# Room accounting of background tasks in a static planner: smaller declared needs, and two pieces more in the bound

## The chip, the cores and the metric

The kernel runs on one NeuronCore of a Trainium2 chip. The metric is the device time of one execution in microseconds (us). Before the change three executions took 2984.54, 2984.85 and 2988.25 us, with a median of 2984.85 us.

## What is computed

One layer of a diffusion block on 2048 latent tokens of width 1024, with 256 context tokens that are read before them. One input projection feeds two groups of four heads each. Group A is an mLSTM matrix memory with chunks of 128 tokens, scanned forward and backward. Group B is gated linear attention (GLA) with chunks of 64 and a decay for each key dimension. Both start from the state that the context leaves. The heads' outputs are normed, gated, put through one output projection and then through a SwiGLU feed-forward part. Cut to what matters:

```python
fc = mixer_features(modulate(rmsnorm(h_ctx, g_mix[l]), shc1, scc1), *proj, 1, h_ctx.shape[1])
fx = mixer_features(modulate(rmsnorm(x, g_mix[l]), shx1, scx1), *proj, rows, GRID_W)
ctx_st = context_states(fc)
ox, _ = mixer_apply(fx, ctx_st, m_norm_g[l], g_norm_g[l], w_out[l])   # both scans, both directions
x = x + gx1 * ox
x = x + gx2 * swiglu(modulate(rmsnorm(x, g_ffn[l]), shx2, scx2), w_gu[l], w_down[l])
return rmsnorm(x, g_final)
```

## The kernel before, in words

The program is straight-line code, written by a Python planner. The foreground is a list of units (`unit(...)`, run by `run_units`): projections whose weights are split into two parts, with 24 matmuls of 512 columns for one unit and one block of 512 tokens. After every such step `after_step` (line 534) calls `tasks_step` (line 508), which lets background tasks write their next piece of code. The tasks are Python generators. A `yield` ends a task's piece for this step.

The background tasks are these, with the function names of the code:
- `bt_task` (kind b) makes the decays' running sums of 256 tokens for four GLA heads and stores them to `d_bt`. Its matmuls use the weights `w2`, which live in the last arena tile.
- `scan_ga` (kind g) makes the attention matrix of one GLA head and 256 tokens ahead of the states, for the first 1024 tokens, and stores it to `d_att`: 16 tasks. `scan_gb` finishes such a piece later. `scan_g` does both for the last 1024 tokens: 16 tasks.
- `state_g` (kind g) makes the states of one GLA head, forward and backward.
- `ctx_gates`, `ctx_state_m`, `ctx_state_g` do the context. `m_tables` (kind m) makes the gate tables of all mLSTM heads, through small round trips over `d_bg` and `d_mp` in memory.
- `state_m` (kind m) makes the states of one mLSTM head in ten steps and a backward pass. It stores them to `d_cf`, `d_ub` and `d_cb`. Head h needs `m_tables`, the context's state, the unit `conv_unit` of its key, and head h-1.
- `scan_m` (kind m) is one mLSTM head on 256 tokens: 32 tasks. Each loads two `d_nm` tables and two `d_wi` tables, a q, a k, a v and two states, and stores its result to `d_hn`.
- `mix` (kind x) joins eight heads' results of 512 tokens for the output projection. It waits for all scans of those tokens.

All of them take their buffers from one pool, `slots`: pieces of 128 by 258 floats, two in each of 16 arena tiles. `take` (line 237) takes the piece that has been free longest and `free` puts it back at the end, so the number of free pieces sets how soon a piece is written again. Thirty pieces are in the pool from the start and one of them holds `rmask` for good. The last arena tile belongs to `w2`; when the last `bt_task` has run, `more_slots` (line 1510) puts its two pieces into the pool.

A task declares how many pieces it may hold (`ROOM`, line 482). `tasks_step` starts a waiting task only if three things hold: its kind has fewer running tasks than `limit`, its dependencies are done, and its room and that of all running tasks together are at most `NSLOT - 3`, which is 29. A task in its last piece (`"tail"`) counts with at most 2. The kinds are gone through in the order f, n, x, b, g, m, and inside a kind by priority: `m_tables` has -1, the states have 0, `scan_ga` 2 or 3, `scan_m` and `scan_g` 4 to 7. The limit of kind g is 4 in the first stage, then 2, then 1 during the gate units, then 2. The limit of kind m is 1, and 2 during the gate units. Kinds b, g and m are held for a step when the planner's own count of VectorE work is more than 8 us (later 5) behind its count of TensorE work.

The order of the foreground is: context and first 1024 tokens of the projections, 38 steps or so; the last 1024 tokens of k, q, kq, v, gv with `conv_unit` in between, up to about 850 us of the trace; 32 steps of `gate_unit`, each with a store to `d_o`; 16 steps of `out_unit`; the feed-forward units; then the same from `out_unit` on for the other 1024 tokens. Loads go through SyncE's queue in the order that the framework's scheduler gives them.

```python
if sum(not x.tail for x in act_) >= limit[kind]:
    break
if t.room + sum(x.room for k in KINDS for x in active[k]) > NSLOT - 3:
    continue
if all(d.done for d in t.deps):
```

Of the kernel before, what the change touches and what calls it, by code (L numbers as in the profile page):

```python
# [43 lines left out]
NSLOT = 32  # L44
# [155 lines left out]
def block_kernel(ctx: ExitStack, tc: tile.TileContext, I, out):  # L200
# [50 lines left out]
    def renew(lo, hi):  # L251

        arena[lo:hi] = [arena_tile(i) for i in range(lo, hi)]
# [225 lines left out]
        modulate(k, ctxv[:, k], ctxv[:, k], TCX, bc_ctx, a1[:, 1], b1[:, 1], hc)  # L479


    ROOM = dict(bt_task=5, ctx_gates=5, ctx_state_g=4, ctx_state_m=5, m_tables=9, state_m=9, state_g=10, scan_m=7, scan_g=8, scan_ga=8, scan_gb=6)
    KINDS = ("f", "n", "x", "b", "g", "m")
    queue = {k: [] for k in KINDS}
    active = {k: [] for k in KINDS}
# [4 lines left out]
    def add(kind, g, *deps, prio=0):  # L490
        t = Task(g, deps, prio, ROOM.get(g.__name__, 0))
        queue[kind].append(t)
        queue[kind].sort(key=lambda t: t.prio)
        return t

    def advance(t):
        if t.wait:
            t.wait -= 1
            return
        try:  # L500
            v = next(t.gen)
            if v == "tail":
                t.tail, t.wait, t.room = True, YT, min(t.room, 2)
            elif v:
                t.wait = v - 1
        except StopIteration:
            t.done = True

    def tasks_step():
        hold[0] -= 1  # L510
        for kind in KINDS:
            if kind in PACED and hold[0] >= 0:
                continue
            act_ = active[kind]
            for t in sorted(act_, key=lambda t: t.prio):
                if kind in PACED and not t.tail and load.behind() > lim[0]:
                    continue
                advance(t)
            act_[:] = [t for t in act_ if not t.done]
            for t in list(queue[kind]):  # L520
                if sum(not x.tail for x in act_) >= limit[kind]:
                    break
                if t.room + sum(x.room for k in KINDS for x in active[k]) > NSLOT - 3:
                    continue
                if all(d.done for d in t.deps):
                    queue[kind].remove(t)
                    act_.append(t)
                    advance(t)
                    if t.done:
                        act_.remove(t)  # L530

    nstep, late, last, hold, lim = [0], [], [None], [0], [LIM]

    def after_step():
        old = pend.pop(0)
        pend.append([])
        for f in old:
            f()
        nstep[0] += 1
        for _ in range(2 if nstep[0] % ADR == 0 else 1):  # L540
            if ada_todo:
                ada_rest(ada_todo.pop(0))
        tasks_step()
        for f in late:
            f()
        late.clear()
# [157 lines left out]
    def bt_task(src, dst):  # L704
# [31 lines left out]
        if not bt_left[0]:  # L736
            more_slots()
# [772 lines left out]
    def more_slots():  # L1510

        renew(NSLOT // 2 - 1, NSLOT // 2)
        slots.extend(arena[-1][:, i] for i in range(2))

    def set_limits(g, m):
        limit["g"], limit["m"] = g, m
# [642 lines left out]
```

## Time and profile before

| | |
|---|---|
| median of three runs | 2984.85 us |
| the profiled execution | 2986.63 us, of which the span is 2984.9 us |
| PE (TensorE matmuls) busy | 2664.0 us, 89% |
| DVE (VectorE) busy | 1939.0 us, 65% |
| ACT (ScalarE) busy | 1355.5 us, 45% |
| POOL (GpSimd) busy | 1786.0 us, 60% |
| granted TensorE clock, mean | 0.945 |

Times in the rows are microseconds from the first instruction unless marked ns. PE is TensorE's matmuls, PEld its weight loads, SP the queue of SyncE that issues loads and stores. PEclk is the granted TensorE clock as a share of 2.4 GHz; the other level is 1.2 GHz. Shares of busy time are averages over stages with different limits, so the stages are read one by one.

### The profile page before, as it was taken

Reading aid. Unit: us, or ns where it says so; the run is one execution under the profiler, and the core shown is the slowest. Engines: PE = TensorE matmul, PEld = TensorE weight load, DVE = VectorE, ACT = ScalarE, POOL = GpSimd, SP = SyncE. Lnnn points to the kernel's source line nnn. Section 1 sums busy time; section 2 is a strip of 40 time slices with the busy share of each in tenths; the row PEclk is TensorE's granted clock in tenths of the full one; section 3 lists DMA queues with packets and bytes.
Section 4 is the critical chain, followed back from the end, with each engine's and each line's share of the span. In section 5 each row is a group of like instructions: output and inputs, shape, how many; then the busy total and the mean of one; then the engine's idle time right before and its main releaser. Section 6 shows DMA issues by size and latency. Waiting matters only on the chain.

```text
span 2984.9 us, 43626 instructions
## 1 busy us (share of the span) xinstructions
PE 2664.0 (89%) x13322; PEld 2229.4 (75%) x13322; DVE 1939.0 (65%) x3949; ACT 1355.5 (45%) x3180; POOL 1786.0 (60%) x2339
## 2 busy tenths in 40 slices
PE   7889898798988886787999999898997999998898
PEld 4778887587776775665777888676786788886777
DVE  7588889886964235668777744767647544447765
ACT  4665555445454444444555433433434333333333
POOL 5667643345455433756667555767766655557773
PEclk7989899899999997898999999999998999999999
DMA  6755433246567767863554422322572332224222
GB/s 256 233 173 168 155 113 112 82 142 206 175 206 211 204 200 186 254 189 97 140 135 131 139 94 85 128 73 81 172 249 83 127 111 84 85 78 143 73 63 85
DMA packets 301817, 426.85 MB, mean 143 GB/s; under 512 B 39310, under 2 KB 186158, under 8 KB 298896
## 3 DMA queue, kind: packets, MB, share of 16 engines
q1 hardware_dynamic: 294224, 405.88, 44.3%
q0 software_dynamic: 7360, 18.19, 1.8%
q8 instruction: 106, 1.74, 0.2%
q14 instruction: 127, 1.04, 0.1%
HBM read 313.38 MB, written 110.55 MB: 142 GB/s over the span
## 4 chain that ended last, share of the span: by engine, by line
PE 42%; DVE 11%; DMA 11%; issue 4%; POOL 3%; ACT 2%; SPq 1%; DVEq 0%; POOLq 0%; ACTq 0%
PE mm L194 39%; DVE area L194 5%; DVE arena L194 3%; DMA arena<-d_nm 3%; DMA arena<-d_wi 2%; PE ps L194 2%; DVE gm L194 2%; DMA d_hn<-arena 1%; POOL w L194 1%; ACT arena L194 1%; SPq L208 1%; DVE xall L194 1%; DMA area<-in_wgu_dram 1%; POOL arena L194 1%; DMA arena<-d_bt 0%
## 5 line engine op out<-in xcount | busy, mean ns | idle before, releaser
L194 PE MATMUL mm<-area,w 128*128 128x512 f32 (+2 forms) x8264 | 2001.4, 400 | 111.5 <-DVE area L194 40.3
L194 PEld LDWEIGHTS mm<-area,w 128*128 128x128 f32 (+1 forms) x8264 | 1562.7, 194 | 457.9 <-DVE area L194 43.1
L194 POOL TENSOR_TENSOR w<-area,w 128x256 fp32r<-128x256 f32 x572 | 455.1, 818 | 272.8 <-ACT w L194 254.1
L194 POOL TENSOR_TENSOR w<-wr,w 128x256 fp32r<-128x256 f32 (+2 forms) x484 | 407.4, 862 | 167.5 <-ACT w L194 151.0
L194 POOL TENSOR_TENSOR arena<-arena 128x128 f32<-128x128 f32 (+1 forms) x520 | 248.7, 502 | 154.6 <-DMA arena<-d_bt 44.6
L194 ACT CAST w<-area 128x512 fp32r<-128x512 f32 x286 | 176.9, 620 | 283.9 <-PE mm L194 257.2
L194 PE MATMUL ps<-arena,arena 128*128 128x129 f32 (+1 forms) x1392 | 215.6, 298 | 72.5 <-ACT arena L194 30.4
L194 PEld LDWEIGHTS ps<-arena,arena 128*128 128x128 f32 x1392 | 195.8, 208 | 96.1 <-ACT arena L194 37.3
L194 DVE TENSOR_TENSOR arena<-arena,arena 128x256 f32<-128x256 f32 (+2 forms) x209 | 143.9, 697 | 188.0 <-DMA arena<-d_wi 90.6
L194 PE MATMUL mm<-w,area 128*128 128x256 f32 x1728 | 245.3, 299 | 6.9 <-ACT gm L194 4.9
L194 DVE TENSOR_TENSOR area<-area 128x512 f32<-128x512 f32 (+2 forms) x230 | 168.9, 747 | 112.5 <-DMA area<-in_wgu_dram 62.1
L194 DVE SCALAR_TENSOR_TENSOR gm<-gm,pc 128x63 f32<-128x63 f32 (+5 forms) x408 | 232.1, 611 | 7.5 <-ACT gm L194 5.1
L194 PEld LDWEIGHTS mm<-w,area 128*128 128x128 f32 x1728 | 229.3, 204 | 8.9 <-ACT gm L194 5.1
L194 ACT CAST w<-wr 128x512 fp32r<-128x512 f32 (+3 forms) x272 | 158.0, 583 | 142.7 <-PE mm L194 70.2
L194 DVE SCALAR_TENSOR_TENSOR area<-mm,modc,area 128x512 f32<-128x512 f32 (+1 forms) x184 | 131.7, 722 | 92.0 <-PE mm L194 91.9
L194 DVE TENSOR_TENSOR gm<-mm,gm 128x512 f32<-128x512 f32 (+3 forms) x136 | 93.0, 684 | 146.3 <-PE mm L194 122.6
L194 ACT COPY gm<-mm 128x512 f32<-128x512 f32 (+3 forms) x215 | 123.0, 574 | 141.5 <-PE mm L194 121.7
L194 PE MATMUL ps<-arena,xall 128*128 128x64 f32 x896 | 129.9, 287 | 35.8 <-DVE xall L194 14.6
L194 PEld LDWEIGHTS ps<-arena,xall 128*128 128x128 f32 x896 | 123.9, 207 | 50.0 <-issue 19.6
L194 DVE TENSOR_TENSOR arena<-ps,arena 64x128 f32<-64x128 f32 x448 | 128.5, 287 | 49.6 <-ACT ps L194 44.1
L194 ACT ACTIVATE ps<-arena 128x256 f32<-128x256 f32 x224 | 85.0, 383 | 161.3 <-DVE xall L194 112.2
L194 DVE TENSOR_TENSOR xall<-ps,arena 64x128 f32<-64x128 f32 x448 | 129.3, 289 | 7.4 <-PE ps L194 0.6
(176 smaller groups left out, 3037.6 us busy)
## 6 DMA issues: line engine op xcount, KB each, us to landing
area<-in_wgu_dram SPq DMA_DIRECT2D x170, 256.0 KB, 2.7
d_ff<-gm SPq DMA_DIRECT2D x88, 256.0 KB, 2.0
arena<-d_ff SPq DMA_DIRECT2D x88, 256.0 KB, 2.8
wr<-in_win_dram SPq DMA_DIRECT2D x72, 256.0 KB, 3.7
area<-in_wada_dram SPq DMA_DIRECT2D x32, 512.0 KB, 4.5
wr<-in_wout_dram SPq DMA_DIRECT2D x64, 256.0 KB, 3.7
arena<-d_kq SPq DMA_DIRECT2D x112, 128.0 KB, 3.0
arena<-d_bt SPq DMA_DIRECT2D x80, 128.0 KB, 3.0
```

The lines of the kernel that those rows point to most:

```text
L194: return f(out, *args, **kw)
L208: return nc.sync.dma_start(o, i)
```

## The change

The declared needs of nine kinds of task become smaller, and the bound becomes a variable that grows by two when `more_slots` gives the pool its last two pieces. No instruction of any task changes; what changes is the step at which a task may start.

```diff
-    ROOM = dict(bt_task=5, ctx_gates=5, ctx_state_g=4, ctx_state_m=5, m_tables=9, state_m=9, state_g=10, scan_m=7, scan_g=8, scan_ga=8, scan_gb=6)
+    ROOM = dict(bt_task=4, ctx_gates=5, ctx_state_g=4, ctx_state_m=4, m_tables=6, state_m=6, state_g=7, scan_m=7, scan_g=7, scan_ga=6, scan_gb=5)
...
-                if t.room + sum(x.room for k in KINDS for x in active[k]) > NSLOT - 3:
+                if t.room + sum(x.room for k in KINDS for x in active[k]) > room_of[0]:
                     continue
...
+    room_of = [NSLOT - 3]
     nstep, late, last, hold, lim = [0], [], [None], [0], [LIM]
...
         renew(NSLOT // 2 - 1, NSLOT // 2)
         slots.extend(arena[-1][:, i] for i in range(2))
+        room_of[0] += 2
```

## Rows read from the trace of the kernel before

**Rows 1.** the page: span, and busy time, share and instructions of each engine

```profile
span 2984.9 us, 43626 instructions
...
PE 2664.0 (89%) x13322; PEld 2229.4 (75%) x13322; DVE 1939.0 (65%) x3949; ACT 1355.5 (45%) x3180; POOL 1786.0 (60%) x2339
```

**Rows 2.** windows by stage: us, PE, PEld, DVE, ACT, POOL busy (x), PEclk, DMA, GB/s

```profile
100.00:360.00 260.00, 227.14 (x1561) 213.58 (x1561) 207.76 (x525) 157.29 (x390) 183.19 (x275) 0.91 0.57 182
360.00:640.00 280.00, 238.28 (x1375) 207.65 (x1375) 242.09 (x565) 133.21 (x287) 115.38 (x176) 0.92 0.35 104
640.00:850.00 210.00, 190.95 (x1079) 164.88 (x1078) 164.88 (x344) 107.62 (x314) 108.13 (x158) 0.98 0.63 190
850.00:1220.00 370.00, 295.38 (x1506) 246.97 (x1505) 150.87 (x468) 168.60 (x542) 172.73 (x275) 0.90 0.71 205
1220.00:1385.00 165.00, 143.08 (x724) 118.31 (x724) 113.08 (x300) 82.12 (x213) 105.61 (x164) 0.95 0.66 195
1385.00:1740.00 355.00, 326.10 (x1695) 274.91 (x1694) 264.38 (x681) 178.69 (x471) 233.34 (x358) 0.95 0.44 128
1740.00:2985.00 1245.00, 1163.63 (x5070) 945.88 (x5068) 725.11 (x957) 479.75 (x872) 811.95 (x853) 0.97 0.33 107
```

**Rows 3.** tiles: DMA of one name, count, issue ns, first and last start us

```profile
L210 SPq DMA_DIRECT2D d_att<-arena x16: 319/326/2007, 182.2 to 620.0; - x16
...
L210 SPq DMA_DIRECT2D d_bt<-arena x32: 319/320/418, 132.1 to 547.1; - x32
...
L208 SPq DMA_DIRECT2D arena<-d_zg x2: 319/371/423, 511.5 to 523.5; - x2
...
L210 POOL DMA_DIRECT2D d_cf<-arena x32: 539/560/596, 662.7 to 1071.6; - x32
...
L210 SPq DMA_DIRECT2D d_cf<-arena x4: 319/350/383, 358.2 to 430.0; - x4
...
L208 SPq DMA_DIRECT2D arena<-d_nm x64: 319/382/806, 865.7 to 1582.8; - x64
```

**Rows 4.** the timeline of DVE and PE at 565 us: start, us, idle before

```profile
565.59 0.24 DVE L194 TENSOR_TENSOR_SCAN arena<-arena,mctx 4x16 f32<-4x16 f32 x1 [9.05 <-DMA arena<-d_bg]
...
566.52 8.41 PE L194 MATMUL mm<-area,w 128*128 128x512 f32 x24 [15.17 <-ACT gm L194]
```

**Rows 5.** prices: PE's timeline (start, us), then DVE's groups of 100:1650 by form

```profile
1186.48 2.50 PE L194 MATMUL ps<-arena,arena 128*128 128x129 f32 x20 [0.95 <-DVE arena L194]
...
1137.31 1.10 PE L194 MATMUL ps<-arena,xall 128*128 128x64 f32 x8 [1.17 <-ACT arena L194]
...
L194 DVE TENSOR_TENSOR xall<-ps,arena 64x128 f32<-64x128 f32 x416 | 120.0, 289 | 6.9 <-PE ps L194 0.6
...
L194 DVE COPY_PREDICATED arena<-lmask,ps 128x256 f32<-128x256 uint8 x204 | 88.9, 445 | 6.1 <-ACT arena L194 1.4 <-PE ps L194 1.3
...
L194 DVE SCALAR_TENSOR_TENSOR arena<-arena,wcb,ps 128x129 f32<-128x129 f32 x60 | 20.6, 344 | 14.2 <-ACT arena L194 11.5 <-DMA d_ub<-arena 1.6
```

**Rows 6.** 850 to 1220 in parts, as Rows 2, and two tiles' DMAs in them

```profile
850.00:1075.00 225.00, 196.24 (x1044) 164.21 (x1043) 87.95 (x260) 103.21 (x327) 114.68 (x184) 0.98 0.70 209
...
1075.00:1150.00 75.00, 53.95 (x262) 44.17 (x260) 26.51 (x86) 31.88 (x110) 25.09 (x42) 0.90 0.69 187
...
1150.00:1220.00 70.00, 45.19 (x202) 38.59 (x203) 36.41 (x122) 33.51 (x107) 32.96 (x49) 0.67 0.76 211
...
L210 SPq DMA_DIRECT2D d_o<-gm x25: 319/382/1386, 857.3 to 1068.3; - x25
...
L208 SPq DMA_DIRECT2D arena<-d_nm x16: 319/382/806, 865.7 to 1049.0; - x16
...
L210 SPq DMA_DIRECT2D d_o<-gm x5: 383/422/422, 1077.2 to 1143.3; - x5
...
L208 SPq DMA_DIRECT2D arena<-d_nm x10: 320/388/488, 1089.6 to 1145.4; - x10
```

**Rows 7.** waits of SP's queue, 850:1220: us in total, times, longest us

```profile
SPq L208 <- DMA d_hn<-arena: 27.5, 14, 5.5
```

## The prediction, made before the change was timed

> **What bounds the kernel now.** I read the page first [rows 1]: PE is busy for 2664 of 2984.9 us and no other engine for more than 65%. So PE sets the time, and what can be won is PE's idle time and the time in which it runs at the lower clock. Then I read the windows by stage [rows 2]. For each stage I call "lost" the idle time of PE plus (1 - PEclk) times the length; this is an upper measure, since the clock is also low while PE idles. It gives 33+23 = 56 us for 100:360, 42+22 = 64 for 360:640, 19+4 = 23 for 640:850, 75+37 = 112 for 850:1220, 22+8 = 30 for 1220:1385 and 29+18 = 47 for 1385:1740. All of these 332 us lie where background tasks run. After 1740 the change can alter nothing but addresses: all scans are over.
>
> The stages have different limits. In 360:640 DVE is busy for 242 of 280 us (86%), in 100:360 for 80%; there the conv and attention work of DVE sets the pace. In 850:1220 DVE is busy for 41% only, and the losses there fall into two halves [rows 6]. From 850 to 1075 25 gate steps pass (25 stores to d_o) at 8.8 us each, with 8 `scan_m` (16 loads of d_nm, two to each) and 29+4.5 us lost: 1.3 us a step. From 1075 to 1150 5 steps pass at 16.5 us each with 5 `scan_m`, and 21+7.5 us are lost: 5.7 us a step. In the first half a `state_m` holds one of the two m places; in the second two `scan_m` run side by side. From 1150 to 1220 the last scans and the first `mix` run, and 25+23 = 48 us are lost.
>
> **What the admission rule does now.** With the old numbers three `scan_ga` and a `bt_task` make 8+8+8+5 = 29, so the limit of four is never used. `m_tables` (9) beside two `scan_ga` and a `bt_task` makes 30, so it waits until the last `bt_task` has gone; the trace agrees, since its gate tables are loaded at 511.5 and 523.5 and the decays' last store is at 547.1 [rows 3]. With the new numbers four `scan_ga` and a `bt_task` make 28, and `m_tables` in its old company makes 6+6+6+4 = 22. So two things move; everything else that runs is held by `limit`, by dependencies or by VectorE's count, which don't change. The two pieces more matter only for tails of 2 that blocked a start for a step or two: counted at nothing, within the bounds below.
>
> **Prices.** PE at full clock takes 2.50/20 = 0.125 us for an f32 instruction of a scan and 1.10/8 = 0.1375 for a level of the attention [rows 5]; each f32 matmul is two instructions, each transpose one. A `scan_ga` has 28 levels' and 4 others: 4.4 us. A `scan_m` has 22: 2.8. A `state_m` has 64+16: 10. A `state_g` has 48: 6. A `scan_g` is a `scan_ga` and 10 more: 5.6. On DVE a `scan_ga` costs 28 x 0.289 + 7 x 0.445 = 11.2 us and a `state_m` 15 x 0.344 for its forward pass and as much again for the other: 10.3 [rows 5]. These amounts are only moved. The PE work of all stages together stays, so the sum is that of the losses, but I write it by stage so that it can be checked.
>
> **100:360, +17 us.** `d_att` is stored 16 times from 182.2 to 620.0 [rows 3]. Four in flight for three lets about three more scans end before 360: +13 us of PE, +34 of DVE. DVE then stands where 360:640 stands now, whose losses are 23% of its length against 21.5% here: +4. Bounds 0 (they fill idle time) to +34 (all of DVE's work on the path). Queued behind each extra scan's POOL subtractions are the weight splits, whose cover is the three weights loaded ahead.
>
> **360:640, -12 us.** These three scans leave (-13 of PE). `m_tables` starts when the third context state has gone: the four store from 358.2 to 430.0 [rows 3], so at about 406. Its wait goes with it: DVE waited 9.05 us for d_bg and PE 15.17 behind it [rows 4]; next to it stands conv work then as now, so I count no gain. Its tables took about 90 us; with seven steps at this stage's pace and the fourth context state behind it, the first `state_m` starts near 490 and not 640, and about 1.3 of them come into this stage (+13 of PE). DVE gets 34 - 13 = 21 us less: its share falls to 79%. The nearest rows with such a share are 100:360 and 640:850, with losses of 21.5% and 11%: between -4 and -34. I take -12.
>
> **640:850, +4 us.** One `state_m` for another, since each waits for the conv unit of its head; two thirds of a `state_g` more. Bounds -2 to +8.
>
> **850:1220, +13 us.** The last store to d_cf is at 1071.6 now [rows 3]. The heads follow their conv units, the last of which ends here at about 800, so I put the end of the last `state_m` eight gate steps into the stage, at some 920. From there two `scan_m` run in each step, for 24 to 25 steps and not for the last 7 to 10. That brings nine more `scan_m` into the stage (25 of PE) and one `scan_g` (6), and takes 1.35 `state_m` and 0.7 `state_g` out (-18): +13. Its losses: 7 steps at 1.3, 25 at x, and a `mix` whose scans end early enough to lie beside gate units, for which I put 15 of the 48. With x = 3.5, the middle between the two halves [rows 6], this is 9+88+15 = 112, as much as now. With x = 1.3 it is 55 less, with 5.7 55 more. No row is nearer: what runs is the second half's, but without `mix` near.
>
> **1220:1740, -40 us.** Nine `scan_m` and a `scan_g` fewer: -31 of PE, and of the 77 us lost here, for 13 `scan_m` and 15 `scan_g` and the start of the feed-forward units, a third of an even share (77/28.5 = 2.7) each, 0.9: -9. Bounds -31 to -58 (2.7 each).
>
> **Sum.** 17 - 12 + 4 + 13 - 40 = -18 us. The profiled execution has 2984.9 us of span and 1.7 around it, 2986.6, which is 1.8 above the median; 2985 - 18 gives 2967 for the median.
>
> **The rivals.** *Slower: two mLSTM scans side by side cost more than they save.* Each loads d_nm and d_wi just before it uses them, into pieces that have just been given back: SP's loads waited 27.5 us in 14 cases for d_hn's stores out of them [rows 7], and the weights of the next gate units are queued behind them on SP. If a step in that company keeps its 5.7 us, the stage is 13+55 = 68 longer, and the sum is +37: 3022. It decides from x = 3.5 + 18/25 = 4.2 on. For it: the row itself. Against it: in 1385:1740, with one `scan_m` beside two `scan_g`, only 47 us are lost in 355. The Trainium skill's page "Perfetto Trace Analysis" (Optimization Strategy) says that the same gap repeating on the engine that should be saturated can mean too little SBUF for the next tile; by that rule more tasks in the same pieces can only add gaps. The wait on d_hn's stores agrees with it. *No change: the room is not what holds.* The `scan_ga` exclude one another level by level (`xbusy`), and VectorE's count skips steps; then the stages before 850 stay as they are, and what is won after 1220 is lost before: within 6 us of now. *Faster still.* Early tables fill DVE-bound stages with work that needs little DVE, and x stays at 1.3: -18 - 55 = -73, 2912. The same page (same section) advises to interleave stages with different limits; [rows 2] show such stages, DVE at 86% and then at 41%, and by it this case would be the likely one.
>
> **How the numbers follow.** A measurement of this kernel can tell about 0.2%, 6 us, from no change. I give 0.42 to the forecast and its neighbourhood (-6 to -50), 0.08 to more, 0.17 to no change and 0.33 to slower. So faster 0.50, same 0.17, slower 0.33. The range goes from 2935 to 3015: it leaves out most of the 0.08 and the upper end of slower, about 0.1. The forecast's own range, without the other sign, is 2935 to 2979.
>
> **What would show it.** Right: the loads of d_zg before 420 and the last store to d_cf near 920; the last store to d_att well before 620; some 55 loads of d_nm between the first d_o store and the last, and not about 36; the last of them near 1400 and not 1582.8; the gate steps at about 12 us each from the end of the `state_m` on. Wrong: gate steps of 14 us and more over the whole second part, with PE's clock there near the 0.90 and 0.67 of the end of the stage now [rows 6]; or a last d_cf store that has hardly moved, which would mean that something other than room held the chain; or more idle PE in 100:360 than the 33 us of now, without a gain in 360:640.

## The result and the profile after

The changed kernel takes 3023.3 us (median of four, 3015.11 to 3025.26), against 2986.55 for the kernel before beside it: a ratio of 1.0114, 95% interval 1.0094 to 1.0134. It is 37 us slower, where 18 us faster was forecast. The profiled execution is the quickest of the four, 3015.11 us with a span of 3013.3, so its trace shows 28.4 of the 37 us. The diff lowers the needs of eight kinds of task, not of nine: those of `ctx_gates`, `ctx_state_g` and `scan_m` stay. The page again, as [rows 1]:

```profile
span 3013.3 us, 43639 instructions
...
PE 2672.7 (89%) x13322; PEld 2236.2 (74%) x13322; DVE 1953.2 (65%) x3949; ACT 1359.4 (45%) x3180; POOL 1785.4 (59%) x2339
```

The windows by stage of the changed kernel, with the columns of [rows 2]: length, busy time of each engine, granted clock, share of the DMA engines, GB/s.

```profile
100.00:360.00 260.00, 227.89 (x1557) 212.68 (x1556) 214.47 (x529) 153.70 (x381) 182.09 (x270) 0.91 0.56 175
360.00:640.00 280.00, 238.52 (x1338) 206.16 (x1337) 235.50 (x562) 144.16 (x334) 116.75 (x191) 0.92 0.41 123
640.00:850.00 210.00, 189.76 (x1125) 165.90 (x1124) 158.24 (x345) 106.93 (x314) 113.11 (x169) 0.98 0.68 201
850.00:1220.00 370.00, 289.81 (x1461) 240.92 (x1460) 155.34 (x484) 163.34 (x523) 152.94 (x230) 0.88 0.70 185
1220.00:1385.00 165.00, 128.70 (x653) 108.87 (x654) 91.82 (x283) 79.88 (x236) 93.65 (x149) 0.86 0.84 218
1385.00:1740.00 355.00, 330.40 (x1678) 276.69 (x1677) 289.50 (x662) 172.87 (x410) 243.45 (x376) 0.97 0.36 114
1740.00:2985.00 1245.00, 1177.20 (x5090) 956.60 (x5089) 721.15 (x933) 484.49 (x876) 815.25 (x859) 0.97 0.33 105
```

The gate units now end inside the fifth window, whose PE clock has fallen from 0.95 to 0.86. The tiles that mark the tasks and the stages, as [rows 3]:

```profile
L210 SPq DMA_DIRECT2D d_att<-arena x16: 319/320/1122, 180.2 to 567.1; - x16
...
L208 SPq DMA_DIRECT2D arena<-d_zg x2: 338/360/383, 404.3 to 404.7; - x2
...
L210 POOL DMA_DIRECT2D d_cf<-arena x32: 542/547/774, 537.4 to 960.2; - x32
...
L208 SPq DMA_DIRECT2D arena<-d_nm x64: 319/382/1407, 837.6 to 1352.9; - x64
...
L210 SPq DMA_DIRECT2D d_o<-gm x32: 319/384/1502, 878.8 to 1297.0; - x32
...
L210 SPq DMA_DIRECT2D d_x<-area x32: 319/327/462, 1302.5 to 2291.5; - x32
```

`m_tables` starts at 404 and not at 511, the last `state_m` ends at 960 and not at 1072, and the last `scan_m` loads at 1353 and not at 1583: the tasks moved as the diff says. In the time that this took, cut at the same places of the foreground in both kernels:

| stretch | before | after | difference |
|---|---|---|---|
| start to the first `d_o` store | 857.3 | 878.8 | +21.5 |
| first `d_o` store to the first `d_x` store (gate units, and the wait for the last scans behind them) | 359.5 | 423.7 | +64.2 |
| first `d_x` store to the first reload of `d_x` (1896.9, 1922.4) | 680.1 | 619.9 | -60.2 |
| from there on | 1088.0 | 1090.9 | +2.9 |

Here is what the second and third of these look like as windows, the kernel before first:

```profile
857.30:1216.80 359.50, 286.04 (x1471) 239.67 (x1472) 143.31 (x449) 164.66 (x532) 165.25 (x262) 0.91 0.71 204
1216.80:1896.90 680.10, 629.28 (x3117) 525.70 (x3116) 444.17 (x1071) 321.58 (x788) 432.79 (x643) 0.96 0.45 133
```

and the changed kernel:

```profile
878.80:1302.50 423.70, 320.16 (x1604) 267.20 (x1603) 171.57 (x547) 190.65 (x611) 183.66 (x269) 0.86 0.75 193
1302.50:1922.40 619.90, 587.18 (x2882) 490.81 (x2881) 416.61 (x931) 283.86 (x653) 399.11 (x602) 0.97 0.38 118
```

The scans that left the later stage gave back 60 us there and cost 64 in the gate stage; in this trace the 21.5 us ahead of it are most of the loss. The column to look at is the last: the gate stage moves about 200 GB/s in both kernels. Length times rate is 73.3 MB before and 81.8 MB after.

### The profile page after: what moved, and what is told of

It reads as the page before. It is cut to its first block, busy times and chain, and to the rows that moved or that the text cites. A ratio compares the mean times of both kernels' runs of the same rounds, so it can differ in the third digit from the quotient of the medians.

```text
span 3013.3 us, 43639 instructions
## 1 busy us (share of the span) xinstructions
PE 2672.7 (89%) x13322; PEld 2236.2 (74%) x13322; DVE 1953.2 (65%) x3949; ACT 1359.4 (45%) x3180; POOL 1785.4 (59%) x2339
## 4 chain that ended last, share of the span: by engine, by line
PE 42%; DVE 7%; issue 2%; POOL 2%; DMA 1%; ACT 1%; DVEq 0%; SPq 0%; POOLq 0%; ACTq 0%
PE mm L194 40%; DVE area L194 4%; PE ps L194 2%; DVE arena L194 1%; POOL w L194 1%; DVE gm L194 1%; POOL area L194 0%; DMA wr<-in_wgu_dram 0%; ACT w L194 0%; DMA gm<-d_x 0%; ACT area L194 0%; DVE xall L194 0%; DVE wr L194 0%; POOL arena L194 0%; POOL sm L194 0%
## 5 line engine op out<-in xcount | busy, mean ns | idle before, releaser
L194 DVE TENSOR_TENSOR arena<-arena,arena 128x256 f32<-128x256 f32 (+4 forms) x210 | 149.5, 721 | 201.5 <-DMA arena<-d_wi 109.4
L194 DVE SCALAR_TENSOR_TENSOR gm<-gm,pc 128x441 f32<-128x441 f32 (+5 forms) x408 | 233.1, 614 | 10.9 <-ACT gm L194 9.3
L194 POOL TENSOR_TENSOR arena<-arena,mneg 128x256 f32<-128x256 f32 x64 | 42.9, 673 | 175.5 <-DMA arena<-d_nm 143.6
```

Of the source, the lines that this page charges most:

```text
L194: return f(out, *args, **kw)
```

## The experiments

Each ratio is against the kernel before on the same chip; the runs were made on several chips, which differ (the kernel before has medians from 2973.6 to 2986.55 us on them), so ratios and not medians are compared between runs. The traces are of one execution each, and stretches of them carry these differences too. Unless a diff says otherwise, a kernel is the changed one with an edit. "Gate stage" is the stretch from the first `d_o` store to the first `d_x` store.

**One m task at a time in the gate stage.**

```diff
-    NGC, NMC = 1, 2
+    NGC, NMC = 1, 1
```

> The changed kernel, with one mLSTM task at a time during the gate units in place of two. Pairs theory (two scan_m side by side make each gate step wait for their tables): the 32 gate steps, 418 us from the first to the last d_o store in the changed kernel, fall to 340 to 360, the PE clock there is back near 0.97, and the scans left over run later at some 4 us each; in all 2985 to 3005. Early theory (the loss lies before 880 us, in the stages that got more scan_ga and m_tables): the gate steps fall too, but the total stays above 3005, since d_o still begins 20 us late and the later scans cost what they saved.

Measured: 2986.05 us, ratio 1.0014 (0.9998 to 1.0031). The early chain stays and the pairs go, and the time is back at that of the kernel before. The late start of the gates stays too (884.4 for 857.3); it is made up by a gate stage that holds fewer `scan_m` than that of the kernel before, 14 for 18. Its gate stage and the stretch behind it:

```profile
884.40:1193.30 308.90, 263.46 (x1363) 220.18 (x1361) 134.41 (x394) 141.82 (x443) 149.99 (x231) 0.95 0.68 199
1193.30:1889.00 695.70, 633.88 (x3123) 530.40 (x3124) 452.91 (x1084) 329.36 (x820) 435.80 (x639) 0.94 0.46 134
```

14 `scan_m` load here inside the stage and 27.5 in the changed kernel. The 13.5 cost (423.7 - 308.9)/13.5 = 8.5 us each inside, and (695.7 - 619.9)/13.5 = 5.6 outside: what is lost by moving one is the difference, 2.9 us.

**The later scans queued only when the gate units are through.** `do(scans_m, range(NH), range(4, 8))` moves to just ahead of the `need` that closes the gate stage.

> The changed kernel, with the scan_m of the last 1024 tokens offered only after the gate units, so that 16 scans and not 28 can run beside the gate units, still two at a time. Pairs theory in the form 'each pair costs the same wherever it runs': the gate steps lose in proportion, 418 falls to some 370, the 16 others cost it back beside the output projection; total 3005 to 3020. Pairs theory in the form 'beside gate units a pair costs 8 us more than one scan beside scan_g': 360 for the gate steps and 2975 to 2995 in all. Early theory: above 3000.

Measured: 2983.03, ratio 1.0001 (0.999 to 1.0013), with 16.5 `scan_m` in a gate stage of 339.6 us. Same reading. The form of the theory in which a pair costs the same wherever it runs (3005 to 3020) is out; the time lies in the other form's range.

**At most one `scan_m` begun in a step.**

```diff
+                if t.gen.__name__ == "scan_m" and began[0] == nstep[0]:
+                    continue
                 if all(d.done for d in t.deps):
```

> The changed kernel, with at most one scan_m started in a step, so that the two that run side by side are a step apart and their eleven loads each don't come in one burst. If the burst is what makes the steps wait: the gate steps fall from 418 to 380 or less and the total to 2980 to 2995. If it is the number of scans in a step, since the mean stays near one a step: 410 to 425, and 3010 to 3025.

Measured: 3013.32, ratio 1.0093 (1.0073 to 1.0113). The gate stage does not shorten (429.6 against 423.7, with 29 `scan_m` in it for 27.5). Lock-step is not what makes the stage long. (A `scan_m` has nine loads, not eleven.)

**Four pieces fewer in the pool, with the same order of the tasks.** Four pieces are taken out of `slots` for good, and the bound stays.

> The changed kernel with four pieces withheld from the pool and the bound kept, so that every task starts at the same step, and only the time between giving back a piece and writing it again is shorter. If loads waiting for pieces just given back (30.7 us of waits for d_hn stores in the gate steps) carry the loss: the gate steps grow by 30 us or more, the total to 3050 or more. If the tables' own time from issue to landing carries it: within 10 us of the changed kernel, 3013 to 3033.

Measured: 3024.26, ratio 1.0139 (1.0119 to 1.0158), beside the changed kernel's 1.0114 (1.0094 to 1.0134). The gate stage is 423.6 us with four pieces fewer, and the waits of SyncE's queue for stores of `d_hn` in it are 29.3 us, against 32.7 in the changed kernel. The prediction's rival had put the pairs' price down to pieces written again too soon: that reason finds no support.

**The two moves one at a time.** The kernel before with the smaller needs for the attention tasks alone, `m_tables` held in its old place:

```diff
-    ROOM = dict(bt_task=5, ..., m_tables=9, ..., scan_ga=8, ...)
+    ROOM = dict(bt_task=4, ..., m_tables=16, ..., scan_ga=6, ...)
```

> The kernel before, in which only scan_ga and bt_task declare their smaller needs (6 and 4), so that four scan_ga run at once as in the changed kernel, while m_tables declares 16 and so keeps its old place behind the last bt_task. The gate stage then holds the old tasks: four state_m and 17 scan_m. Theory of the pairs (the loss is the 11 scan_m that the early chain of the m tasks brings into the gate stage, and the gates' late start is that chain's own work moved ahead of them): gates begin near the 857.3 of before, the time is within 6 us of before, 2980 to 2992. Rival, four attention tasks at once make the stage of 400 to 520 us slower: gates begin 15 to 22 us later, and the time is 3000 to 3010.

Measured: 2992.24, ratio 1.0034 (1.0023 to 1.0044). The other half, the changed kernel with three attention tasks at once:

```diff
-    ROOM = dict(bt_task=4, ..., scan_ga=6, ...)
+    ROOM = dict(bt_task=5, ..., scan_ga=8, ...)
```

> The changed kernel with scan_ga and bt_task back at 8 and 5, so that three scan_ga run at once as before; m_tables and the state_m stay early (13 to 21 steps ahead of before), and 27 scan_m start in the gate stage in place of 29. Theory of the pairs: the gate stage stays about 80 us longer than before's and less than that comes back later, 3008 to 3028. Rival, the four attention tasks carry the loss: gates begin near 860 and the time is 2980 to 2998.

Measured: 2990.72, ratio 1.0028 (1.0014 to 1.0042). Neither theory had this: each half loses a third of a per cent and both together 1.1. The gates begin at 836.6 with four attention tasks alone, 20.7 us earlier than before, and at 864.2 with the early chain alone, 6.9 later; together 21.5 later. Why the two add up so badly ahead of the gates is not settled. What the first half won there it lost again: its gate stage, with 18 `scan_m` as before, is 18.8 us longer. It also moves more:

```profile
836.60:1214.90 378.30, 295.89 (x1517) 249.49 (x1515) 152.79 (x470) 173.72 (x566) 178.71 (x281) 0.89 0.73 205
```

378.3 us at 205 GB/s are 77.6 MB, 4.3 more than before, and at 205 GB/s these would take 21 us (an estimate).

**The loads one step ahead of their use.**

```diff
             Ds.append(Dt)
             Ws.append(W)
+        yield
+        for d in range(2):
...
```

> The changed kernel, in which a scan_m issues its six first loads one step before it uses them (one more yield between them and the additions on GpSimd). The task lasts a step longer, and so 19 scan_m start in the gate stage in place of 29, as the planner counts. By the price of a scan_m inside the gate stage (8.8 us: 418.2 - 294.6 over 27 - 13 scans, changed kernel against the one with one m task at a time) and outside it (5.4 us: 695.7 - 619.9 over the same 14), ten fewer inside are worth 34 us: 2990. Theory that the landing time of the tables makes a scan_m dear: PE's idle time in the gate stage falls further, below 0.8 us for each scan, and the time is 2955 to 2980. Rival, the tables' landing does not matter, since PE waits for the chain of small steps behind them: 2985 to 3000.

Measured: 2986.5, ratio 1.0015 (1.0002 to 1.0027), the rival's number. The gate stage takes 328.7 us for 67.7 MB (206 GB/s), the rate of the kernel before. The stage was no quicker for what it moved; it only moved less. But the edit is no test of the landing, since the step of lead did not hide it. The waits of DVE for `d_wi` in the gate stage (us in total, times, longest), in the changed kernel and in this one:

```profile
DVE arena L194 <- DMA arena<-d_wi: 97.5, 35, 7.0
...
DVE arena L194 <- DMA arena<-d_wi: 63.9, 24, 6.1
```

Over 27.5 and 18 `scan_m` that is 3.5 us for each in both.

**Plain rows in place of the tables.**

```diff
-            dma(chunks(Dt), d_nm[None, r0:r0 + 2].broadcast_to([P, 2, P]))
-            dma(chunks(W), d_wi[None, r0:r0 + 2].broadcast_to([P, 2, P]))
+            dma(chunks(Dt), I["ident"][:, None, :].broadcast_to([P, 2, P]))
+            dma(chunks(W), I["ident"][:, None, :].broadcast_to([P, 2, P]))
```

> The changed kernel, in which the loads of d_nm and d_wi (two rows handed to all 128 partitions) read 128 rows of a constant matrix in their place, of the same size into the same pieces, and the exponentials have no per-row bias; the mLSTM scans therefore compute something else, and no load waits for the tables' making. Order and count of the tasks stay. Theory that the landing time of these broadcast loads (6.0 to 6.6 us in the gate stage) makes a pair of scan_m dear: the loads land in about 3 us, waits of GpSimd and VectorE on them fall to less than half of 117.5 and 93.5 us, the gate stage is 30 to 60 us shorter, and the time is 2965 to 2995. Rival, landing is hidden or as slow with plain rows: 3012 to 3028.

Measured: 2946.53, ratio 0.9869 (0.9846 to 0.9893): 2.45 points of the ratio, some 73 us, below the changed kernel and quicker than the kernel before. The DMA issues of 850:1300 in the changed kernel (tile, queue, count, size of one, median us from issue to landing):

```profile
arena<-d_wi SPq DMA_DIRECT2D x56, 128.0 KB, 6.4
arena<-d_nm SPq DMA_DIRECT2D x55, 128.0 KB, 6.6
arena<-d_cf SPq DMA_DIRECT2D x28, 129.0 KB, 5.2
```

and in this one:

```profile
arena<-in_ident_dram SPq DMA_DIRECT2D x125, 128.0 KB, 3.7
...
arena<-d_cf SPq DMA_DIRECT2D x32, 129.0 KB, 3.3
```

The same number of bytes lands in little more than half the time, and other loads land sooner too.

**Sixteen copies of the tables.** The tables are stored sixteen times, and each group of eight partitions reads a copy of its own:

```diff
-        dma(d_nm, Mr[:, P:2 * P])
+        dma(d_nm.rearrange("j p t -> p j t"), Mr[:, None, P:2 * P].broadcast_to([P, NCP, P]))
...
-            dma(chunks(Dt), d_nm[None, r0:r0 + 2].broadcast_to([P, 2, P]))
+                src = d_t[:, r0:r0 + 2].rearrange("j r t -> j (r t)")
+                dma(t, src[:, None].broadcast_to([NCP, P // NCP, HB]))
```

> The changed kernel, in which m_tables stores d_nm and d_wi sixteen times, 64 KB each, and the load of a scan_m takes each group of eight partitions from a copy of its own in place of all 128 partitions from one place. The result stays that of the reference. Theory that the time of the tables' loads comes from 128 partitions reading the same rows: they land in about 3.7 us as the plain loads did, in place of 6.4 and 6.6, the gate stage is 60 to 70 us shorter than 418.2, and the time is 2945 to 2965, faster than the kernel before. Rival, what was gained with the plain loads came from the other data or from the missing bias of the exponentials (so not from the source addresses): landing stays above 5.5 us and the time is 3010 to 3035, the sixteenfold stores adding some us.

Measured: 2951.11, ratio 0.9925 (0.9909 to 0.994). The loads of the tables in 850:1300:

```profile
arena<-d_wi SPq DMA_DIRECT2D x62, 128.0 KB, 3.1
arena<-d_nm SPq DMA_DIRECT2D x62, 128.0 KB, 3.2
```

So it is the 128 partitions reading one place that is slow, not the data, the size or the missing bias. In the kernel before, with copies:

> The kernel before with the same sixteen copies. Theory that the slow landing costs only where two scan_m run side by side: five steps of 16.5 us fall to the 11 or so of their neighbours and the end of the gate stage gains a little, 2955 to 2970, so that with quick tables the change of the room is worth a little or nothing. Rival, every scan_m pays for its tables wherever it runs: 32 times 2.6 us (69.5 us of the gate stage over 27 scans with the plain loads), some 2900, and the change of the room loses with quick tables too. Rival, nothing but the source of the plain loads' gain was data: 2980 to 2995.

Measured: 2920.75, ratio 0.9821 (0.9804 to 0.9838), the quickest of the versions that leave nothing out, and quicker than both kernels. Scans pay for their tables wherever they run: of the 69.8 us by which the gate stage and the stretch behind it are shorter in the traces (317.0 for 359.5 and 652.8 for 680.1), 27.3 lie behind the gates. The change of the room stays 30 us (1 point of the ratio) behind with quick tables too. With one m task at a time:

> The changed kernel with one m task at a time during the gate units, and sixteen copies of the tables. By the theory that the tables' landing costs in pairs, this gains less by the copies than the changed kernel does: 2950 to 2978 (2986 without copies). If every scan_m pays wherever it runs, it gains as much as the changed kernel, some 75 us: 2905 to 2920.

Measured: 2926.74, ratio 0.9834 (0.9815 to 0.9854); it gains 1.8 points by the copies and the changed kernel 1.9. And the kernel before with plain rows:

> The kernel before, in which the loads of d_nm and d_wi read 128 rows of a constant matrix in their place, of the same size, and the exponentials have no per-row bias; the mLSTM scans therefore compute something else. Against the changed kernel with the same loads (2946.5) it gives the price of the change without slow tables. Theory that only pairs pay: 2955 to 2975, so the change would have won some 10 to 25 us. Rival, every scan pays: 2900 to 2920, and the change would have lost even so.

Measured: 2907.99, ratio 0.9781 (0.9767 to 0.9796), against 0.9869 with the change. My theory that only pairs pay for slow tables fell twice: they are a cost of their own, and what the change loses is something else. Both kernels with copies, the changed one first:

```profile
874.80:1243.60 368.80, 299.48 (x1613) 249.95 (x1611) 173.72 (x547) 190.76 (x612) 183.20 (x267) 0.93 0.72 220
1243.60:1859.70 616.10, 585.73 (x2879) 490.30 (x2879) 419.32 (x932) 285.46 (x655) 400.77 (x604) 0.98 0.37 120
```

and the kernel before with copies:

```profile
851.50:1168.50 317.00, 274.56 (x1469) 229.53 (x1469) 142.65 (x450) 164.61 (x534) 168.77 (x262) 0.94 0.75 230
1168.50:1821.30 652.80, 616.43 (x3114) 517.52 (x3113) 451.44 (x1069) 319.93 (x785) 438.50 (x643) 0.97 0.44 139
```

The gate stage costs 51.8 us more and the later one gives back 36.7. It also moves more again: 81.1 MB against 72.9.

**The same added loads at two places.** On the kernel before with copies, two pieces more are loaded in each of 32 steps and given back unread:

```diff
         nstep[0] += 1
+        if 101 <= nstep[0] < 101+32:
+            for b in range(2):
+                t = take()
+                dma(t, d_kT[0, :, hs_(b)])
+                free(t)
```

> The kernel before with sixteen copies (2920.75), in which each of the 32 steps of the gate units loads two more pieces of 128 KB from d_kT and gives them back unread: 8.4 MB, about what six scan_m load and store (ten transfers of 128 KB each), and no other work. Theory that the gate stage is short of transfers (its DMA engines are busy for 0.74 of the time, against 0.36 after the sixteenth d_x store): PE loses in the gate stage what six more scan_m would cost there by the two kernels with copies, 3.5 us each ((97.0 - 59.8) over 10.5 scans), so some 20 us, and the time is 2935 to 2950. Rival, a scan_m is dear there for its chain of small steps on GpSimd, ScalarE, VectorE and TensorE, not for its transfers: within 8 us, 2913 to 2929.

Measured: 2947.93, ratio 0.989 (0.9873 to 0.9907), 0.69 points or 20 us above the kernel without them. In the later place (140 in place of 101):

> As the kernel with two more loads in each gate step, but in the 32 steps from the sixth behind the gate units' last on. Theory of the transfers: where the DMA engines are busy for 0.36 the same loads cost 0 to 7 us (1.1 us for each of six scan_m there), 2918 to 2930, and less than half of what they cost in the gate stage. Rival, the loads cost through the order of SyncE's queue or through the pieces that they hold, which is the same in both places: as much as in the gate stage, within 5 us.

Measured: 2932.89, ratio 0.9845 (0.9821 to 0.9868), 0.24 points or 7 us, whose interval still meets that of no added loads. The windows of the first:

```profile
853.80:1210.10 356.30, 289.71 (x1474) 245.29 (x1473) 151.16 (x455) 166.09 (x533) 168.94 (x262) 0.90 0.76 230
1210.10:1857.60 647.50, 615.83 (x3114) 517.42 (x3113) 449.88 (x1069) 319.06 (x787) 433.84 (x644) 0.98 0.44 140
```

and of the second:

```profile
855.40:1175.30 319.90, 277.41 (x1467) 233.30 (x1467) 140.83 (x450) 164.11 (x534) 168.37 (x262) 0.93 0.75 229
1175.30:1837.60 662.30, 617.77 (x3114) 515.36 (x3113) 451.99 (x1069) 318.56 (x785) 432.51 (x643) 0.97 0.47 150
```

64 loads of 128 KB are 8.4 MB. In the gate stage the rate stays at 230 GB/s and the share of the DMA engines at 0.75 to 0.76; what gives is the length, by 39.3 us, and 8.4 MB at 230 GB/s are 36.5. In the later stage the rate rises from 139 to 150 GB/s and the length by 9.5 us. But the trace without added loads is of another chip and of the quickest of its four executions (2913.1 us, median 2920.75). Held against each other, the two kernels with loads, which ran on one chip, put the price at 36.4 us in the gate stage (356.3 and 319.9) and 14.8 in the later one (662.3 and 647.5). By the ratios it is 20 us and 7 of the whole time, and their difference of 0.45 points, 13 us, has an interval of 5 to 22. So loads without any work lengthen the gate stage, and by more than the later one (two to three times by these numbers); that is shown. That the DMA engines' rate is what they run into is not.

SyncE's queue and the pieces are not ruled out as causes, since the same loads do not meet the same queue in both places. Its waits for the landing of loads of `d_kT`, of which the gate stage without added loads has none (us in total, times, longest), in the gate stage of the first and in the later stage of the second:

```profile
SPq L208 <- DMA arena<-d_kT: 39.3, 24, 3.3
...
SPq L208 <- DMA arena<-d_kT: 25.1, 22, 2.1
```

These waits are of the edit's own making. And added up from the trace, SyncE spends about 194 of the 317.0 us of the gate stage issuing (415 loads and stores) without the added loads and 224 of 356.3 with them, but only 187 of 652.8 in the later stage without them. This queue is a rival to the engines' rate, and no run parts the two. From issue to landing the loads of the gate stage take much the same without the added loads and with them: 4.0 and 3.6 us for `d_nm`, 3.2 and 3.5 for `d_wi`, 3.4 and 3.6 for `d_kT`.

**One start in a step, with copies.**

> The changed kernel with sixteen copies (2951.11), in which only one scan_m may start in a step, so that the two that run side by side are a step apart and not in lock-step. Theory that two chains at the same point of their course collide on the engines: the gate stage loses 15 us or more less than 97, 2925 to 2938. Rival, the loss is the same in any phase, as without copies, where the same edit gave 3013.3 for 3023.3: 2940 to 2952.

Measured: 2946.16, ratio 0.9882 (0.986 to 0.9904), 0.43 points below the same kernel without the rule. Its gate stage is 367.4 us, against 368.8; in its profile the gain lies behind the gate stage (605.9 for 616.1). The theory of colliding chains wanted it in the gate stage.

**Copies, and the loads a step ahead, in the kernel before.**

> The kernel before with sixteen copies, in which a scan_m issues its six first loads one step before it uses them. If GpSimd's and VectorE's waits on the tables still hold TensorE, 2900 to 2912. If the landing is covered by now, the longer task costs as much as it brings (15 scan_m in the gate stage in place of 17, the last start at step 194 in place of 174): 2915 to 2930.

Measured: 2934.9, ratio 0.9848 (0.983 to 0.9867), slower than copies alone if anything: 8 us, with an interval of 1 to 16. The theory's gain did not come, but the landing was not covered by the lead: DVE waits 35.9 us for `d_wi` in the gate stage with 15 `scan_m`, and 23.3 with 18 in the kernel without the lead.

## Why the prediction was wrong

Gate stages side by side. The MB are length times GB/s of the windows, so the last column is the rate turned over:

| kernel | gate stage, us | GB/s | DMA share | MB | us per MB |
|---|---|---|---|---|---|
| one m task at a time | 308.9 | 199 | 0.68 | 61.5 | 5.02 |
| loads a step ahead | 328.7 | 206 | 0.74 | 67.7 | 4.86 |
| later scans after the gates | 339.6 | 206 | 0.71 | 70.0 | 4.85 |
| before | 359.5 | 204 | 0.71 | 73.3 | 4.90 |
| four attention tasks only | 378.3 | 205 | 0.73 | 77.6 | 4.87 |
| after | 423.7 | 193 | 0.75 | 81.8 | 5.18 |
| early chain only | 436.8 | 199 | 0.72 | 86.9 | 5.03 |
| copies, one m task | 282.6 | 217 | 0.70 | 61.3 | 4.61 |
| copies, before | 317.0 | 230 | 0.75 | 72.9 | 4.35 |
| copies, after | 368.8 | 220 | 0.72 | 81.1 | 4.55 |
| copies, before, loads added | 356.3 | 230 | 0.76 | 81.9 | 4.35 |

The other gate stages lie between 4.22 (kernel before, plain rows) and 5.18 us per MB (four pieces fewer). So the length follows the MB within some 7 to 9%, with slow tables and with quick ones, whatever the tasks are. This alone does not show that the stage is bound by its transfers, because each task brings work along with its MB; SyncE's issues go with the length as well (416 in the gate stage before and 496 after, 0.86 and 0.85 us for each). A `scan_m` has ten transfers, nine loads (one each of k, q and v, and two each of both tables and the states) and one store, together 1.31 MB: at 204 GB/s 6.4 us, an estimate, where the run with one m task measures 8.5 in the gate stage and 5.6 in a later stage whose DMA share is 0.38 to 0.46. My 2.8 us of PE are less than half of either.

What the runs with added loads support is the difference between the two places. By the ratios 64 loads cost 13 us more in the gate stage than later, which for the ten transfers of a `scan_m` makes 2.1 us (an estimate, with an interval of 0.7 to 3.4). With copies, one m task at a time takes 13.5 `scan_m` out of the gate stage and the kernel gains 0.91 points, 27 us: 2.0 each. The price of the loads is thus of the size of what the second `scan_m` loses there.

Point by point:

**850:1220, +13 us: the step that failed.** Its count of tasks held: 54 loads of `d_nm` between the first and the last `d_o` store, for 55 foretold, the last at 1353 for 1400, the last `d_cf` store at 960 for 920. Its price did not. I gave a step with two `scan_m` x = 3.5 us of lost PE time, the middle of two halves [rows 6], though the nearest row said 5.7. The last 16 gate steps show it (changed kernel, from the 16th `d_o` store to the last):

```profile
1012.00:1297.00 285.00, 202.12 (x1015) 168.60 (x1013) 112.32 (x385) 127.27 (x413) 111.58 (x159) 0.83 0.78 188
```

PE idles for 82.9 of 285 us at a clock of 0.83: by the prediction's own measure 82.9 + 0.17 x 285 = 131 us over 16 steps, 8.2 a step. The steps take 17.8 us each, past the 14 that the prediction had named as the sign of being wrong. The whole stage grew by 64 us where 13 were forecast.

- **The number that was there.** The two last columns of [rows 2] stand at 0.71 and 205 GB/s in 850:1220 and at 0.44 and 128 in 1385:1740, and I used neither. Nine more `scan_m` are 9 x 1.31 = 11.8 MB, 58 us at 205 GB/s (an estimate from that row). With 58 in place of 13 the forecast would have been +27. The stage's MB rose by less, 8.5, since `state_m` and `state_g` left it: some 41 us at 205 GB/s (an estimate). The other 23 of its 64 us came with a lower rate, 193, and are not explained.
- **The rival that came true gave the right number (+37) for the wrong reason.** The number is in part luck: the rival's +68 for the gate stage stands against 64.2, but its +9 ahead of it was 21.5 and its -40 behind it -60.2, and these errors cancel in part. As the reason it had the pairs wait for pieces in use [rows 7]. Four pieces fewer changed nothing that is clear of the intervals. The Trainium skill's page "Perfetto Trace Analysis" (Optimization Strategy) holds that a repeating gap can mean too little SBUF; this case's measurement speaks against it here, with a ratio of 1.0139 against 1.0114 and a gate stage of 423.6 against 423.7 us.
- **1220:1740, -40 us** was -60.2: the scans that left took more than their 2.8 us and 0.9 of loss with them, some 5.6 us each. Why they cost that much in a stage with transfers to spare is not shown.
- **100:360, +17, 360:640, -12, 640:850, +4: +9 in all, and 21.5 measured.** Of the three scans more before 360 one came (nine stores of `d_att` by then for eight), and by 400 the lead was gone: ten have been issued by the last `d_zg` store in both kernels, and that store comes at 401.7 for 398.5. PE's busy time from 100 to 850 is the same in both (656.4 and 656.2 us, the three windows added). So these stages were not relieved; they did as much, part of it work of the m chain moved ahead, and the gates began later by it.
- **`m_tables` at 406** started at 404.3. Its stall moved with it, as foreseen: DVE waits 9.78 us for `d_bg` at 431, for 9.05 before.
- **Interleaving.** The Trainium skill's page "Perfetto Trace Analysis" (Optimization Strategy) also says that interleaving stages with different limits may help; moved this way, the work here made the kernel 1.1% slower. I had judged the limits by DVE (86% and 41%). The stage into which the work went had DVE to spare, but was the dear one for loads.

What stays open: whether the loads in the gate stage run into the rate of the DMA engines or into SyncE's queue; why the two moves cost 21.5 us ahead of the gates where one alone gains 20.7 and the other costs 6.9; and 12.5 us by which the changed kernel with copies is longer in the gate stage than the kernel before with copies and as many bytes added (368.8 against 356.3).

## What to carry to other kernels

Price a task that you move by each resource of the stage that receives it, its bytes over the GB/s of that window and its issues on the loading queue included, and not only by the engine that is busiest over the whole kernel. A stage whose rate stays put while its length changes may be short of loads, even where its DMA share reads 0.7 and not 1.0; the same added loads, put in two stages, tell whether loads are dear in one of them. Hold such traces against each other on one chip, and against the change of the whole time, before a stage's difference is called a price. And where loads hand a few rows to all partitions, look at their landing beside that of plain loads of the same size.

## What the runs showed of the hardware

- A load of 128 KB in which 128 partitions read the same 1 KB of memory took a median of 6.0 us (kernel before, `d_nm`, 850:1300) to 6.6 (changed kernel) from issue to landing; over the gate stages of all nine kernels with one copy the medians of `d_nm` and `d_wi` lie between 4.2 and 6.6. With sixteen copies they lie between 2.8 and 4.0, and with 128 different rows at 3.6 and 3.7. Here sixteen copies were worth 1.8 points of the kernel's time (0.9821). How much of this is the wait for the tables and how much the stage's rate (204 to 230 GB/s) is not parted.
- With about 130-KB transfers mixed with stores, the busy share of the DMA engines lay between 0.68 and 0.78 over the gate stages of all runs (0.78 with plain rows, at 235 GB/s). The Trainium skill's page "Perfetto Trace Analysis" (Identifying the Most-Contended Engine) warns that occupancy misleads for the DMA engines; this trace agrees in so far as 8.4 MB more made a stage at 0.75 longer, by 36 to 39 us in the traces and by 20 in the whole time.
